# One encoder layer on one core: the Newton factor on ScalarE, and q and k scaled head by head

## The chip, the core and the metric

One core of a Trainium2 chip runs the whole layer. The core has TensorE (matrix products, PE in the profile; its weight loads are PEld), VectorE (DVE), ScalarE (ACT), GpSimd (POOL) and SyncE (SP, here only a queue of DMA issues). Each engine works through its own instructions in order and waits on semaphores for the others. The metric is the device time of one execution in microseconds (us), lower is better.

## The reference

A transformer layer on 1024 tokens of width 1024: a modulated RMS norm, one input projection, two attentions beside each other (a 2-D neighbourhood attention with 8 heads, and a dilated sliding-window attention with 12 heads in three groups), a gated merge, and a SwiGLU network. What bears on the change is the norm of q and k, over the 64 elements of a head:

```python
def rms_norm(x, g):
    x32 = x.astype(f32)
    y = x32 * lax.rsqrt(jnp.mean(x32 * x32, axis=-1, keepdims=True) + EPS)
    return (y * g.astype(f32)).astype(x.dtype)

qa = rms_norm(qa.reshape(b, s, NA_HEADS, HEAD_DIM), g_qa[l])
ka = rms_norm(ka.reshape(b, s, NA_HEADS, HEAD_DIM), g_ka[l])
...
qb = partial_rotary(rms_norm(qb.reshape(b, s, DIL_HEADS, HEAD_DIM), g_qb[l]), pos)
kb = partial_rotary(rms_norm(kb.reshape(b, s, DIL_HEADS, HEAD_DIM), g_kb[l]), pos)
```

## The kernel before

The projection to q, k and v is cut into ten units of two heads each. Units 0 to 3 are plain ("stage A" in what follows): for each of eight blocks of 128 tokens, TensorE accumulates 128 x 384 columns (q, k, v of two heads) in a bank of PSUM `pd`. Units 4 to 9 go in pairs ("stage B"): the products of two units and two token halves are formed from seven products of mixed operands instead of eight, and sums (`acc`, kept where `hT` lay) are put together by VectorE. Every float32 operand is split into a high part (`whi`, by a ScalarE copy, L129 or L1164) and a low part (`wlo`, by a subtraction, on GpSimd at L1170, on VectorE or GpSimd at L132); three matrix products replace one.

Each block of a unit ends in a post, `proj_post`, 80 in all: 32 in stage A (`acc is None`) and 48 in stage B. A post holds q and k of two heads as `qn`, 128 tokens x 4 x 64. ScalarE squares it (`sq`, L371), VectorE sums over 64 (`ss`, L375). ScalarE makes a first inverse root y as exp(-ln(ss/64 + eps)/2) (`rv`, L377 and L378), since it is not exact enough, and its square (`ry`, L379). VectorE then makes z = (ss + 64 eps) y^2 (`rz`, L380), from which one Newton step is y (1.5 - z/128). Here it is (z - 192) y (L381), times -1/128: in stage A that factor was put in when `qn` was copied out of PSUM (L373), in stage B it stands in the last product. That product (L384 or L386) takes all four heads at once, the 128x4 factor being broadcast over the 64 elements. For the dilated units GpSimd then turns 16 of the 64 elements (`ra`, `rb`, L393 to L396).

Behind the posts, TensorE transposes `qn` (L437), VectorE and ScalarE write its high and low parts (`qk`, L463 to L466), and the attention of the unit before runs between the pieces of the projection: scores (`ps_s`, L539 or L606), mask and minimum on VectorE (L553, L616, tile `st` or `sx`), exp on ScalarE (L554, L618), transposes (L565, L631), copies `PT` (L569, L638), and the product with v. VectorE also accumulates the modulation of later parts (`acc`, L337 and L339) in that time. `smix` are mixed operands fetched by DMA.

The order of TensorE's instructions is written out by hand. In this part of the program the order on VectorE, ScalarE, GpSimd and SyncE is set by a scheduler that estimates each instruction's time and follows priorities; `proj_post` has a raised one. So an edit there can move its neighbours. Behind about 600 us come the merge, the output projection and the SwiGLU network, which hold no posts.

Of the kernel before, what the change touches and what calls it, by code (L numbers as in the profile page):

```python
# [12 lines left out]
AF = mybir.ActivationFunctionType  # L13
ALU = mybir.AluOpType
# [34 lines left out]
def hybrid_layer(ctx: ExitStack, tc: tile.TileContext, x, colp, wada1, wada2, bada2, wqkv, wg, wpa, wpb,  # L49
                 wo, w1, w2, hgain, ropeg, rope, rbias, bmask, g2r, out):  # L50
    nc = tc.nc
# [47 lines left out]
    for i in (0, 2):  # L99
        nc.vector.scalar_tensor_tensor(hg[:, i:i + 1], hg[:, i:i + 1], 0.125, hg[:, i + 1:i + 2],  # L100
                                       op0=ALU.mult, op1=ALU.mult)
# [251 lines left out]
    def urgent(off):  # L353
        def deco(f):
            def g(*a):
                with tc.high_priority(off):
                    return f(*a)
            return g
        return deco

    @urgent(PP)
    def proj_post(U, t, pd=None, acc=None, here=False):
        pd = U.pd[t] if pd is None else pd
        qn = ap_.tile([128, 4, 64], F32, tag="qn", bufs=9, name="qn")
        U.qn[t] = qn
        pq = pd[:, :256].rearrange("p (h d) -> p h d", h=4)
        if acc is not None:
            nc.vector.tensor_add(qn, acc[:, :256].rearrange("p (h d) -> p h d", h=4), pq)
        v_out(U, t, pd, acc, here)
        sq = ap_.tile([128, 256], F32, tag="sq", bufs=1, name="sq")  # L370
        nc.scalar.activation(sq, pd[:, :256] if acc is None else qn.rearrange("p h d -> p (h d)"), AF.Square)  # L371
        if acc is None:
            nc.scalar.activation(qn, pq, AF.Copy, scale=-1.0 / 128)  # L373
        ss = ap_.tile([128, 4], F32, tag="ss4", bufs=2, name="ss4")
        nc.vector.tensor_reduce(ss, sq.rearrange("p (h d) -> p h d", h=4), axis=mybir.AxisListType.X, op=ALU.add)  # L375
        y, y2, z, r = (ap_.tile([128, 4], F32, tag=g, bufs=3, name=g) for g in ("rv", "ry", "rz", "rz"))
        nc.scalar.activation(y, ss, AF.Ln, scale=1.0 / 64, bias=eps)  # L377
        nc.scalar.activation(y, y, AF.Exp, scale=-0.5)  # L378
        nc.scalar.activation(y2, y, AF.Square)  # L379
        nc.vector.scalar_tensor_tensor(z, ss, 64 * EPS, y2, op0=ALU.add, op1=ALU.mult)  # L380
        nc.vector.scalar_tensor_tensor(r, z, -192.0, y, op0=ALU.add, op1=ALU.mult)  # L381
        rr = r[:, :, None].to_broadcast([128, 4, 64])
        if acc is None:
            nc.vector.tensor_tensor(qn, qn, rr, op=ALU.mult)  # L384
        else:
            nc.vector.scalar_tensor_tensor(qn, qn, -1.0 / 128, rr, op0=ALU.mult, op1=ALU.mult)  # L386
        if U.kind < 3:
            ra = ap_.tile([128, 4, 16], F32, tag="ra", bufs=2, name="ra")
            rb = ap_.tile([128, 4, 16], F32, tag="rb", bufs=2, name="rb")
            tb = U.tab[:, t]  # L390
            v4 = lambda z: z.rearrange("p (a b) c -> p a b c", a=2)
            tv = lambda f, c0, c1: tb[:, f, :, None, c0:c1].to_broadcast([128, 2, 2, c1 - c0])
            nc.gpsimd.tensor_tensor(v4(ra), v4(qn[:, :, 0:16]), tv(0, 0, 16), op=ALU.mult)  # L393
            nc.gpsimd.tensor_tensor(v4(rb[:, :, 0:8]), v4(qn[:, :, 8:16]), tv(1, 0, 8), op=ALU.mult)
            nc.gpsimd.tensor_tensor(v4(rb[:, :, 8:16]), v4(qn[:, :, 0:8]), tv(1, 8, 16), op=ALU.mult)
            nc.gpsimd.tensor_tensor(qn[:, :, 0:16], ra, rb, op=ALU.add)  # L396

    def v_out(U, t, pd, acc, here):
        if U.kind == 0:
            nc.scalar.activation(U.v[:, t, :], pd[:, 256:384], AF.Copy)  # L400
            return
        vs = acc[:, 256:384] if here else ap_.tile([128, 128], F32, tag="vs", bufs=3, name="vs")
        if acc is None:
            nc.scalar.activation(vs, pd[:, 256:384], AF.Copy)
        else:
            nc.vector.tensor_add(vs, acc[:, 256:384], pd[:, 256:384])
        vd = v_d[U.u - 2]
        if U.kind == 3:
            nc.scalar.dma_start(vd.rearrange("(c r j) d -> r j c d", c=8, r=16)[2 * t:2 * t + 2], vs)
        else:  # L410
            nc.scalar.dma_start(vd[t * 128:(t + 1) * 128, :], vs)
# [656 lines left out]
    for t in range(6):  # L1068
        proj_post(U, t)
# [13 lines left out]
    def plain_unit(u):  # L1083
        s = len(stream)
        if u > 1:
            for k in range(KT):
                def load(k=k):
                    raws[u, k] = unit_load(u, k, True)

                def split(k=k):  # L1090
                    nextw[u, k] = wsplit(raws[u, k], nc.vector if k > 1 and k % 2 else None)

                when(s - 64 + 8 * k, load)
                when(s - 36 if k < 2 else s - 8 + k, split)

        def job(t, k):
            U = unit_of(u, [nextw[u, kk] for kk in range(KT)])
            proj_chunk(U, t, k)
            if k == KT - 1:
                proj_post(U, t)  # L1100

        for t in range(8):
            for k in range(KT):
                stream.append(lambda t=t, k=k: job(t, k))
# [5 lines left out]
    def pair_evac(nm, t, pd, ua, ub):  # L1110
        if not sums:
            sums.extend(spare(q, 1536, F32) for q in range(2))
        A, B = (z[:, 384 * t:384 * t + 384] for z in sums)
        p = pd[:, :384]
        if nm == "p2":
            proj_post(unit_of(ua), t, pd, A)
        elif nm == "x4":
            proj_post(unit_of(ua), 4 + t, pd, B)
        elif nm == "w22":
            proj_post(unit_of(ub), t, pd, A, True)  # L1120
        else:
            with tc.high_priority(PP):
                if nm == "p1":
                    nc.scalar.activation(A, p, AF.Copy)
                elif nm == "x1":
                    nc.vector.tensor_add(B, A, p)
                elif nm == "x2":
                    nc.vector.tensor_add(A, A, p)
                    nc.vector.tensor_add(B, B, p)  # L1129
                else:  # L1130
                    nc.vector.tensor_add(A, A, p)
            if nm == "x3":
                proj_post(unit_of(ub), 4 + t, pd, B, True)
# [875 lines left out]
```

## Time and profile before

| | |
|---|---|
| median of 3 runs | 1483.48 us (1482.39 to 1486.61) |
| profiled execution, its own time | 1483.91 us |
| its span | 1482.1 us |
| TensorE clock granted, mean | 0.995 |
| busy: PE, DVE, ACT, POOL | 1454.2, 1112.4, 709.8, 734.3 us |
| posts | 80, from 58 to 502 us |

A row on instructions gives line, engine, operation, out<-in by the program's names, the shape, and "xN", then total busy us and the mean of one in ns, then the idle time of the engine ahead of them and what ended it; or, for one line of the code, shortest/median/longest in ns and the first and last start. A row on waits, "A <- B: us, times, longest", says that an engine stood idle ahead of A until B was done. Busy time of an instruction includes the time in which it was issued but held back by another engine.

### The profile page before, as it was taken

Reading aid. Unit: us, or ns where it says so; the run is one execution under the profiler, and the core shown is the slowest. Engines: PE = TensorE matmul, PEld = TensorE weight load, DVE = VectorE, ACT = ScalarE, POOL = GpSimd, SP = SyncE. Lnnn points to the kernel's source line nnn. Section 1 sums busy time; section 2 is a strip of 40 time slices with the busy share of each in tenths; the row PEclk is TensorE's granted clock in tenths of the full one; section 3 lists DMA queues with packets and bytes.
Section 4 is the critical chain, followed back from the end, with each engine's and each line's share of the span. In section 5 each row is a group of like instructions: output and inputs, shape, how many; then the busy total and the mean of one; then the engine's idle time right before and its main releaser. Section 6 shows DMA issues by size and latency. Waiting matters only on the chain.

```text
span 1482.1 us, 24530 instructions
## 1 busy us (share of the span) xinstructions
PE 1454.2 (98%) x8024; PEld 1238.8 (84%) x8024; DVE 1112.4 (75%) x2144; ACT 709.8 (48%) x1807; POOL 734.3 (50%) x706
## 2 busy tenths in 40 slices
PE   9999999999899999999999999999999999999998
PEld 7999998898788777888888888888888888888886
DVE  6788868878578874684877596878777777599568
ACT  5665665665678865465422353322222233354442
POOL 0353466664353544346521402677767776104464
PEclk9999999999899999999999999999999999999999
DMA  9657686775666866864374325344533334898353
GB/s 354 241 174 238 202 269 234 238 230 175 208 189 208 259 211 218 300 247 131 118 251 150 104 88 178 122 149 164 176 101 107 107 107 152 278 348 302 113 157 100
DMA packets 190416, 285.17 MB, mean 192 GB/s; under 512 B 29616, under 2 KB 91728, under 8 KB 189520
## 3 DMA queue, kind: packets, MB, share of 16 engines
q1 hardware_dynamic: 171712, 269.96, 55.0%
q10 hardware_dynamic: 18576, 13.64, 2.8%
q8 instruction: 64, 1.05, 0.3%
q14 instruction: 64, 0.52, 0.1%
HBM read 218.67 MB, written 64.86 MB: 191 GB/s over the span
## 4 chain that ended last, share of the span: by engine, by line
PE 66%; DVE 2%; issue 0%; ACT 0%; DVEq 0%
PE ps_v L1645 8%; PE ps_d L1645 8%; PE ps_s L1645 7%; PE ps_t L1645 6%; PE ps_d L840 6%; PE ps_s L1844 4%; PE ps_d L1844 4%; PE ps_t L1844 3%; PE ps_v L1844 3%; PE ps_s L1580 2%; PE ps_d L1580 2%; PE ps_v L1580 1%; PE ps_v L840 1%; PE ps_v L1431 1%; PE ps_t L1431 1%; PE ps_t L840 1%
## 5 line engine op out<-in xcount | busy, mean ns | idle before, releaser
L129 ACT ACTIVATE whi<-raw 128x512 fp32r<-128x512 f32 (+2 forms) x265 | 158.2, 608 | 178.8 <-PE ps_s L1844 37.1
L132 DVE TENSOR_TENSOR wlo<-raw,whi 128x512 fp32r<-128x512 f32 (+1 forms) x171 | 149.5, 892 | 47.5 <-ACT whi L129 44.3
L132 POOL TENSOR_TENSOR wlo<-raw,whi 128x512 fp32r<-128x512 f32 (+2 forms) x94 | 128.3, 1372 | 109.3 <-ACT whi L129 108.9
L350 PE MATMUL ps_d<-whi,hT 128*128 128x384 f32 x384 | 101.2, 338 | 0.0
L1595 POOL TENSOR_TENSOR e<-e,c 128x512 f32<-128x512 f32 x44 | 68.9, 1565 | 60.1 <-DVE c L1725 35.9
L1202 PE MATMUL ps_d<-whi,hT 128*128 128x384 f32 x328 | 94.2, 347 | 3.3 <-DVE hT L1129 2.0
L129 ACT ACTIVATE whi<-ws 128x512 fp32r<-128x512 f32 x60 | 37.7, 628 | 120.2 <-DVE ws L1662 87.1
L840 PE MATMUL ps_d<-hT,whi 128*128 128x512 f32 x256 | 81.8, 400 | 0.0
L132 POOL TENSOR_TENSOR wlo<-m,whi 128x512 fp32r<-128x512 f32 x35 | 50.7, 1455 | 52.3 <-ACT whi L129 52.3
L1202 PE MATMUL ps_d<-whi,smix 128*128 128x384 f32 x224 | 66.3, 353 | 7.8 <-DMA smix<-t_d 4.9
L1593 ACT ACTIVATE e<-e 128x512 f32<-128x512 f32 x44 | 27.4, 630 | 94.8 <-DVE e L1728 66.9
L1170 POOL TENSOR_TENSOR wlo<-raw,whi 128x384 fp32r<-128x384 f32 x48 | 51.1, 1079 | 40.0 <-ACT whi L1164 35.4
L350 PEld LDWEIGHTS ps_d<-whi,hT 128*128 128x128 f32 x384 | 69.6, 188 | 0.6 <-issue 0.6
L618 ACT ACTIVATE P<-P,st 128x256 f32<-128x256 f32 (+2 forms) x100 | 45.7, 459 | 43.2 <-DVE st L616 43.1
L1202 PEld LDWEIGHTS ps_d<-whi,hT 128*128 128x128 f32 x328 | 61.4, 192 | 4.6 <-DVE hT L1129 2.7
L350 PE MATMUL ps_d<-wlo,hT 128*128 128x384 f32 x192 | 64.2, 334 | 0.0
L1170 POOL TENSOR_TENSOR wlo<-chain,whi 128x384 fp32r<-128x384 f32 x36 | 37.5, 1055 | 49.1 <-ACT whi L1164 47.2
L1645 PE MATMUL ps_d<-h2T,whi 128*128 128x512 f32 x200 | 61.7, 389 | 0.0
L1645 PE MATMUL ps_v<-h2T,whi 128*128 128x512 f32 x192 | 59.2, 389 | 0.0
L1645 PE MATMUL ps_s<-h2T,whi 128*128 128x512 f32 x192 | 59.1, 389 | 0.0
L132 POOL TENSOR_TENSOR wlo<-gl,whi 128x512 fp32r<-128x512 f32 x30 | 40.0, 1348 | 35.1 <-ACT whi L129 35.1
L1202 PE MATMUL ps_d<-wlo,hT 128*128 128x384 f32 x164 | 55.7, 339 | 0.0
(479 smaller groups left out, 4652.9 us busy)
## 6 DMA issues: line engine op xcount, KB each, us to landing
raw<-in_w_dram SPq DMA_DIRECT2D x139, 256.0 KB, 3.5
raw<-in_wqkv_dram SPq DMA_DIRECT2D x116, 192.0 KB, 4.1
ga_d<-e SPq DMA_DIRECT2D x77, 256.0 KB, 2.5
raw<-ga_d SPq DMA_DIRECT2D x77, 256.0 KB, 3.1
smix<-t_d SPq DMA_DIRECT2D x64, 256.0 KB, 4.0
wa<-in_wada_dram SPq DMA_DIRECT2D x24, 512.0 KB, 5.1
m<-in_w_dram SPq DMA_DIRECT2D x44, 256.0 KB, 5.2
hT<-t_d SPq DMA_DIRECT2D x40, 256.0 KB, 4.8
```

The lines of the kernel that those rows point to most:

```text
L129: h = nc.scalar.activation(hi[:, :n], r, AF.Copy)
L132: (eng or nc.gpsimd).tensor_sub(lo[:, :n], r, fview(hi[:, :n]))
L350: nc.tensor.matmul(pd[:, :384], tok(a, k, t), U.w[k][b][:, :384], start=(k == 0 and i == 0), stop=(k == KT - 1 and i == 2))
L618: nc.scalar.activation(C.P[h][:nq, c], C.P[h][:nq, c], AF.Exp, scale=-1.0, bias=nm, accum_out=sm)
L840: nc.tensor.matmul(pb, w[x][:, k * 128:(k + 1) * 128], b[y][k], start=(k == 0 and q == 0), stop=(k == 3 and q == 2))
L1170: nc.gpsimd.tensor_sub(lo[:, :384], z, fview(hi[:, :384]))
L1202: nc.tensor.matmul(pd[:, :384], lhs, w[k][b][:, :384], start=(k == 0 and i == 0), stop=(k == 3 and i == 2))
L1431: nc.tensor.matmul(pb, w[a][:, j * 128:(j + 1) * 128], oT[pr][:, b, hs], start=(j == 0 and q == 0), stop=(j == len(prs) - 1 and q == 2))
L1580: nc.tensor.matmul(pbs[hf], h2T[a][:, k, t * 128:(t + 1) * 128], wow[hf, k][b], start=(n == 0 and (a, b) == PASS[0]), stop=(n == KT - 1 an ...
L1595: nc.gpsimd.tensor_mul(sg, sg, up)
L1645: nc.tensor.matmul(pb, w[p][:, k * 128:(k + 1) * 128], b[q][:, k], start=(k == 0 and i == 0), stop=(k == 3 and i == 2))
L1844: nc.tensor.matmul(pb[m], o[0][a][:, m * 128:(m + 1) * 128], o[1][b], start=(k == 0 and i == 0), stop=(k == HT - 1 and i == 2))
```

## The change

The Newton factor 1.5 - z/128 is made by a ScalarE copy with a scale and a bias (`r`, tile `rz`, L381 of the new file). `qn` is then multiplied head by head by two scalars of each partition, r and y, in one instruction for each head: four tensor_scalar of 128x64 in place of one product of 128x256 with a broadcast. The copy of `qn` out of PSUM loses its factor. The new file is three lines shorter from there on, so L1161, L1125, L1126 and L403 below are L1164, L1128, L1129 and L406 of the file before.

```diff
         if acc is None:
-            nc.scalar.activation(qn, pq, AF.Copy, scale=-1.0 / 128)
+            nc.scalar.activation(qn, pq, AF.Copy)
...
         nc.vector.scalar_tensor_tensor(z, ss, 64 * EPS, y2, op0=ALU.add, op1=ALU.mult)
-        nc.vector.scalar_tensor_tensor(r, z, -192.0, y, op0=ALU.add, op1=ALU.mult)
-        rr = r[:, :, None].to_broadcast([128, 4, 64])
-        if acc is None:
-            nc.vector.tensor_tensor(qn, qn, rr, op=ALU.mult)
-        else:
-            nc.vector.scalar_tensor_tensor(qn, qn, -1.0 / 128, rr, op0=ALU.mult, op1=ALU.mult)
+        nc.scalar.activation(r, z, AF.Copy, scale=-1.0 / 128, bias=1.5)
+        for h in range(4):
+            nc.vector.tensor_scalar(qn[:, h], qn[:, h], r[:, h:h + 1], y[:, h:h + 1], op0=ALU.mult, op1=ALU.mult)
```

TensorE's instructions stand in the same order as before. On the other engines the scheduler puts them in a new one. Three places in the first pair of units, where stage B begins; `ss_3493` of before is `ss_3589` of now, and so on through `ss_3552`/`ss_3651`, `ss_3656`/`ss_3758` and `ss_3708`/`ss_3813`: the sums of squares of four posts that follow each other.

First, VectorE at the first post of these four, before:

```order
L375 TENSOR_REDUCE ss_3493<-sq 128x4
L368 TENSOR_TENSOR qn<-hT,ps_d 128x256
L406 TENSOR_TENSOR vs<-hT,ps_d 128x128
L380 SCALAR_TENSOR_TENSOR rz<-ss_3493,ry 128x4
L381 SCALAR_TENSOR_TENSOR rz<-rz,rv 128x4
L386 SCALAR_TENSOR_TENSOR qn<-qn,rz 128x256
L375 TENSOR_REDUCE ss_3552<-sq 128x4
```

And now:

```order
L375 TENSOR_REDUCE ss_3589<-sq 128x4
L368 TENSOR_TENSOR qn<-hT,ps_d 128x256
L403 TENSOR_TENSOR vs<-hT,ps_d 128x128
L380 SCALAR_TENSOR_TENSOR rz<-ss_3589,ry 128x4
L375 TENSOR_REDUCE ss_3651<-sq 128x4
L383 TENSOR_SCALAR qn<-qn,rz,rv 128x64 x4
```

The next post's reduction has moved into the gap in which ScalarE makes the factor, and four instructions stand where one stood.

Second, VectorE at the third and fourth post, before:

```order
L380 SCALAR_TENSOR_TENSOR rz<-ss_3656,ry 128x4
L375 TENSOR_REDUCE ss_3708<-sq 128x4
L339 SCALAR_TENSOR_TENSOR acc_3692<-wa_3690,cact,acc_3692 128x512
L381 SCALAR_TENSOR_TENSOR rz<-rz,rv 128x4
L1128 TENSOR_TENSOR hT<-hT,ps_s 128x384
L1129 TENSOR_TENSOR hT<-hT,ps_s 128x384
L339 SCALAR_TENSOR_TENSOR acc_3692<-wa_3690,cact,acc_3692 128x512
L386 SCALAR_TENSOR_TENSOR qn<-qn,rz 128x256
L380 SCALAR_TENSOR_TENSOR rz<-ss_3708,ry 128x4
```

And now:

```order
L380 SCALAR_TENSOR_TENSOR rz<-ss_3758,ry 128x4
L1125 TENSOR_TENSOR hT<-hT,ps_d 128x384
L1126 TENSOR_TENSOR hT<-hT,ps_d 128x384
L339 SCALAR_TENSOR_TENSOR acc_3797<-wa_3795,cact,acc_3797 128x512
L380 SCALAR_TENSOR_TENSOR rz<-ss_3813,ry 128x4
L383 TENSOR_SCALAR qn<-qn,rz,rv 128x64 x4
```

The z of the third post is now further back, behind the evacuation that came after it, and the z of the fourth still stands behind a second evacuation and a step of `acc`.

Third, ScalarE at the same two posts, before:

```order
L377 ACTIVATE rv<-ss_3656,eps 128x4
L378 ACTIVATE rv<-rv 128x4
L379 ACTIVATE ry<-rv 128x4
L371 ACTIVATE sq<-qn 128x256
L411 DMA v_d<-vs 128x128
L377 ACTIVATE rv<-ss_3708,eps 128x4
L378 ACTIVATE rv<-rv 128x4
L379 ACTIVATE ry<-rv 128x4
L1164 ACTIVATE whi<-raw 128x384 x4
```

And now:

```order
L377 ACTIVATE rv<-ss_3813,eps 128x4
L378 ACTIVATE rv<-rv 128x4
L379 ACTIVATE ry<-rv 128x4
L381 ACTIVATE rz<-rz 128x4 x2
L1161 ACTIVATE whi<-raw 128x384 x4
```

The factors of both posts stand one after the other ahead of the four copies that make the high parts of the next weights, and the second needs the z of the fourth post.

## The prediction

> **What bounds the kernel now.** I read first the page's busy times, then the busy time of each engine in two stretches cut where the changed line runs (its 80 instances start between 61.9 and 500.0 us), then who waits for whom there.
>
> ```profile
> PE 1454.2 (98%) x8024; PEld 1238.8 (84%) x8024; DVE 1112.4 (75%) x2144; ACT 709.8 (48%) x1807; POOL 734.3 (50%) x706
> core 0: us, PE busy (x) PEld busy (x) DVE busy (x) ACT busy (x) POOL busy (x), PEclk, DMA share, GB/s
> 55.00:206.00 151.00, 151.00 (x1054) 143.99 (x1053) 118.80 (x326) 97.16 (x351) 71.91 (x146) 1.00 0.67 204
> 206.00:503.00 297.00, 277.41 (x2028) 249.04 (x2026) 233.76 (x712) 195.76 (x658) 167.20 (x207) 0.98 0.68 214
> ```
>
> TensorE bounds the whole. In stage A (55 to 206 us, 32 posts of the plain units) it never idles. In stage B (206 to 503 us, 48 posts of the paired units) it idles 19.6 of 297 us, which is most of the 28 us that it idles at all. VectorE is busy 118.8 of 151 us in A and 233.8 of 297 us in B, 79% in both: the next engine in line, executing in order. What TensorE waits for in B:
>
> ```profile
> PE ps_d L1202 <- DMA smix<-t_d: 4.9, 4, 2.9
> PE ps_d L1202 <- issue: 4.0, 2, 2.7
> PE ps_s L1202 <- DVE st L616: 3.2, 3, 1.9
> PE ps_d L1202 <- DVE hT L1129: 2.0, 2, 1.8
> PE ps_t L301 <- DVE PT L638: 1.1, 1, 1.1
> ```
>
> Columns are total us, times, longest. Three of these five name VectorE, 6.3 us: already now VectorE is at moments too late, behind its own queue. So in B VectorE time is not free. In A TensorE has no wait at all, so there VectorE time has cover. And VectorE's own idle time is in good part waiting for ScalarE (the first four rows from stage B, then two from stage A without its first 20 us):
>
> ```profile
> DVE ss L375 <- ACT sq L371: 12.9, 19, 2.8
> DVE qk L465 <- ACT qk L464: 6.5, 12, 0.9
> DVE rz L380 <- ACT ry L379: 4.5, 7, 1.2
> DVE sx L556 <- ACT P L554: 2.5, 7, 0.6
> ...
> DVE rz L380 <- ACT ry L379: 10.9, 10, 2.5
> DVE ss L375 <- ACT sq L371: 6.8, 8, 1.6
> ```
>
> **What the change removes and adds on VectorE.** Removed are one 128x4 product (L381) and one 128x256 product (L384 in A, L386 in B) for each post. First the rows of B, then those of A, then shortest, median and longest of single instructions over the whole run:
>
> ```profile
> L386 DVE SCALAR_TENSOR_TENSOR qn<-qn,rz 128x256 f32<-128x256 f32 x48 | 30.9, 644 | 0.9
> L381 DVE SCALAR_TENSOR_TENSOR rz<-rz,rv 128x4 f32<-128x4 f32 x48 | 22.0, 458 | 1.1
> L380 DVE SCALAR_TENSOR_TENSOR rz<-ss,ry 128x4 f32<-128x4 f32 x48 | 17.8, 372 | 4.5 <-ACT ry L379 4.5
> ...
> L384 DVE TENSOR_TENSOR qn<-qn,rz 128x256 f32<-128x256 f32 x32 | 15.7, 489 | 1.6
> L381 DVE SCALAR_TENSOR_TENSOR rz<-rz,rv 128x4 f32<-128x4 f32 x32 | 6.3, 196 | 0.6
> ...
> L381 DVE SCALAR_TENSOR_TENSOR rz<-rz,rv x80: 145/164/1224, 61.9 to 500.0; 128x4 f32<-128x4 f32 x80
> L380 DVE SCALAR_TENSOR_TENSOR rz<-ss,ry x80: 147/163/1065, 61.4 to 498.9; 128x4 f32<-128x4 f32 x80
> L386 DVE SCALAR_TENSOR_TENSOR qn<-qn,rz x48: 406/425/1453, 230.0 to 501.3; 128x256 f32<-128x256 f32 x48
> L384 DVE TENSOR_TENSOR qn<-qn,rz x32: 409/425/1184, 62.1 to 205.5; 128x256 f32<-128x256 f32 x32
> L375 DVE TENSOR_REDUCE ss<-sq x80: 396/416/422, 58.7 to 496.6; 128x4 f32<-128x256 f32 x80
> ```
>
> The means are far above the shortest, while the reduction L375 never is. One place shows why, VectorE's three rows first, then GpSimd's:
>
> ```profile
> 228.15 0.88 DVE L380 SCALAR_TENSOR_TENSOR rz<-ss,ry 128x4 f32<-128x4 f32 x1
> 229.07 0.93 DVE L381 SCALAR_TENSOR_TENSOR rz<-rz,rv 128x4 f32<-128x4 f32 x1
> 230.04 1.18 DVE L386 SCALAR_TENSOR_TENSOR qn<-qn,rz 128x256 f32<-128x256 f32 x1
> ...
> 228.00 2.94 POOL L1170 TENSOR_TENSOR wlo<-chain,whi 128x384 fp32r<-128x384 f32 x3
> ```
>
> Three GpSimd instructions of 0.98 us run one after the other, and each of the three VectorE instructions ends just after one of them: the two engines take turns, instruction by instruction. So what counts is also how many such instructions VectorE issues.
>
> Added are four tensor_scalar of 128x64 with two scalars per partition. No such shape is in the trace. The nearest rows, and two of the last of them back to back:
>
> ```profile
> L251 DVE TENSOR_SCALAR xd<-ident,xs x4: 281/284/288, 9.3 to 13.5; 128x128 f32<-128x128 f32 x4
> L337 DVE TENSOR_SCALAR acc<-wa,cact x6: 477/478/586, 77.2 to 308.5; 128x512 f32<-128x512 f32 x6
> L969 DVE TENSOR_SCALAR yT<-yT,sc x16: 535/546/1106, 22.5 to 54.1; 128x512 f32<-128x512 f32 x16
> ...
> 27.85 1.00 DVE L969 TENSOR_SCALAR yT<-yT,sc 128x512 f32<-128x512 f32 x2
> ```
>
> L251 and L337 have one scalar operand: (477 - 281)/384 = 0.51 ns an element. L969 has two: 535 - 477 = 58 ns more. So 128x64 with two is 281 - 64 x 0.51 + 58 = 306 ns. Two L969 end after 1.00 us, not 1.09, so the next starts 0.09 us before the end of one. Four occupy 4 x (0.306 - 0.09) = 0.86 us of VectorE, undisturbed. L969 also reaches 1106 ns, so tensor_scalar takes turns with GpSimd too.
>
> With the turns, stage B: the old pair costs 0.458 + 0.644 - 0.08 (overlap) = 1.02 us. The turn costs 0.31 us at L381 (458 - 145), 0.24 at L386 (644 - 406), 0.22 at L380 (372 - 147). I take 0.24 for each of the four, L386 being the instruction that they replace: 0.86 + 4 x 0.24 = 1.82 us, +0.80 a post, 48 x 0.80 = +38 us. Ends: no turns at all gives 0.86 - 1.02 = -0.16, or -8 us; 0.31 for each gives +1.08, or +52 us. Stage A: old 0.196 + 0.489 - 0.08 = 0.60; turns cost 0.05 (L381) to 0.08 (L384), so new 0.86 + 4 x 0.06 = 1.10, +0.50 a post, +16 us over 32 posts (ends +8 and +19).
>
> [...]
>
> **What it adds as waits.** The factor goes to ScalarE: 80 more ACTIVATE of 128x4, like L379:
>
> ```profile
> L379 ACT ACTIVATE ry<-rv x80: 188/206/238, 61.1 to 498.4; 128x4 f32<-128x4 f32 x80
> ```
>
> 80 x 0.206 = 16.5 us on an engine that is busy 293 of 448 us in A and B together: the duration itself is covered by its idle time. But the path is now VectorE, ScalarE, VectorE where it was VectorE alone. In 25 of the 80 posts the order puts the tensor_scalar right behind the z instruction, so VectorE stands for the whole trip; elsewhere a reduction or other work lies between. The new wait is unknown: its nearest rows are those of 4.5 us (L380) and 12.9 us (L375) in B; I take 9 in B, and 6 in A by the number of posts. Ends 0 and 13 each. On ScalarE the new instruction stands in front of others: in 23 posts it is directly ahead of the copies L1164 that make the weights' high parts, on which GpSimd (L1170) and then TensorE wait. At the third place of the order shown above two of them now precede four such copies:
>
> ```profile
> 240.17 1.75 ACT L1164 ACTIVATE whi<-raw 128x384 fp32r<-128x384 f32 x4
> 240.75 4.54 POOL L1170 TENSOR_TENSOR wlo<-raw,whi 128x384 fp32r<-128x384 f32 x4 [1.65 <-ACT whi L1164]
> 243.39 0.96 DVE L380 SCALAR_TENSOR_TENSOR rz<-ss,ry 128x4 f32<-128x4 f32 x1
> 249.08 0.33 PE L1202 MATMUL ps_d<-whi,hT 128*128 128x384 f32 x1
> ```
>
> The copies started at 240.17 and TensorE used the result from 249.08; GpSimd was done at 245.3, so 3.8 us of room. The second z ran at 243.39 to 244.35; behind it the copies start 4.2 us later, and the room is gone by 0.4 us. I put +4 us for such places in B, with 0 and +20 as ends (20 is 21 product starts at about 1 us each).
>
> The dropped scale of the copy L373 and the merged branches change no instruction's size: nothing. TensorE's order is unchanged; SyncE's differs by a few neighbours that swap places, priced at nothing since the landings they carry are needed many us later; if that cover fails it shows as more of the 4.9 us wait for smix.
>
> **The sum.** Stage B: VectorE 233.8 + 38 = 272 us of work, plus its waits for ScalarE 12.9 + 6.5 + 4.5 + 2.5 = 26 us, plus the new 9: 307 us in a stretch of 297, so +10. (Its waits for TensorE I let go: they vanish when VectorE is late.) Stage A by the same sum: 118.8 + 16 + 17.7 + 6 = 158.5 of 151, +7.5; but TensorE never waits there, and such waits shrink when VectorE falls behind, so I take +4. ScalarE's queue +4. Together +18 us on the profiled execution's 1483.9 us (its span is 1482.1; the median of the runs is 1483.48): **1502 us**. What is late next, after VectorE, are the weights' low parts on GpSimd.
>
> **Rivals.** (1) VectorE and the chain both overflow: 0.31 us a turn (+52), waits 13 in B gives 234 + 52 + 26 + 13 = 325, +28; A its full +7.5; ScalarE's queue +10: 1529 us. For it: turns cluster, as at 228 us; against it: GpSimd is busy only 56% of B. (2) It stays hidden: ScalarE's waits on the VectorE side melt by 26 us as VectorE falls behind, and 272 fits in 297: 1484 to 1488 us. The same time comes out if the four cost what the pair costs, 0.255 us each in B. For it: TensorE has 100% in A; against it: 6.3 us of waits for VectorE already now, and the prices above. [...] (3) Faster: the tensor_scalar are short enough to slip between GpSimd's instructions. Then VectorE gains 8 us in B and up to the 6.3 us of TensorE's waits for it go: about 1478 us. It decides where four of them occupy less than the 1.02 us of the old pair, under 0.255 us each; undisturbed they take 0.215, so this needs a turn cost under 0.04 us, where the rows show 0.22 to 0.31.
>
> **Chances.** My case (1490 to 1515 us) 0.52, rival 1 0.18, rival 2 0.18, rival 3 0.12. The likeliest gives 1502. About 0.3%, 4.5 us, is what a measurement of this kernel can tell from no change. Slower: 0.52 + 0.18 + a small part of rival 2 = 0.73; same 0.15; faster 0.12. The range from 1480 to 1530 leaves out most of rival 3 and the part of rival 1 beyond 1529, near 0.18.
>
> **What would show it.** In the profile after: 320 tensor_scalar with a shortest near 0.30 us and a mean in B near 0.5; VectorE busy near 272 us in what was stage B; a new row of VectorE waiting for ScalarE's rz; more TensorE idle, named st, hT, PT or whi, before 520 us; from then on the same lengths as now. I am wrong if the tensor_scalar take under 0.25 us, if TensorE's idle time in B stays near 20 us with VectorE above 90%, or if the change in time comes from behind 503 us.

## The result, and the profile after

The changed kernel takes 1520.32 us (median, 1513.53 to 1525.81) where the kernel before took 1483.11 us on the same chip: a ratio of 1.0249, 95% interval 1.0219 to 1.0279. It is slower, by 37 us. The profiled execution took 1521.67 us, its span is 1519.9 us. Its first line on the page, and the busy time of the engines in four stretches, first of the changed kernel, then of the kernel before (columns as in the first fence of the prediction). The cuts are the first plain projection, the first and the last matmul of the paired projections, and the first matmul of the merge:

```profile
PE 1468.8 (97%) x8024; PEld 1246.0 (82%) x8024; DVE 1158.5 (76%) x2304; ACT 720.6 (47%) x1887; POOL 734.8 (48%) x706
61.50:202.20 140.70, 139.52 (x987) 132.28 (x986) 123.40 (x366) 92.72 (x350) 71.01 (x140) 1.00 0.65 198
202.20:528.00 325.80, 287.69 (x2002) 256.01 (x2001) 261.06 (x790) 197.94 (x695) 158.85 (x206) 0.95 0.62 197
528.00:725.60 197.60, 194.94 (x1078) 155.38 (x1077) 131.19 (x264) 116.17 (x261) 107.98 (x81) 1.00 0.67 230
725.60:1519.90 794.30, 789.61 (x3525) 652.95 (x3523) 602.77 (x781) 281.07 (x508) 392.14 (x269) 1.00 0.48 160
```

```profile
60.50:199.70 139.20, 139.20 (x986) 132.19 (x985) 113.12 (x313) 89.79 (x325) 69.19 (x142) 1.00 0.66 201
199.70:494.00 294.30, 274.92 (x2001) 248.80 (x2000) 228.78 (x699) 192.87 (x652) 161.96 (x205) 0.98 0.69 218
494.00:688.00 194.00, 193.79 (x1079) 155.30 (x1078) 127.74 (x249) 115.05 (x254) 107.11 (x81) 1.00 0.67 233
688.00:1482.10 794.10, 789.46 (x3524) 652.58 (x3523) 602.64 (x781) 279.34 (x506) 391.45 (x268) 1.00 0.48 160
```

The second column is the length. The start is 1.0 us later, the plain stretch 1.5 longer, the paired stretch 31.5, the next one 3.6, the rest 0.2: together 37.8 us, the difference of the spans. So five sixths of the loss are in the paired stretch. There TensorE idles 38.1 us where it idled 19.4, and the same 2000 matmuls or so keep it busy 12.8 us longer. The mean granted clock, third from the end, is 0.95 there, against 0.98.

The added instructions: the groups of the paired stretch and of the plain one, then all instances of each with shortest, median and longest:

```profile
L383 DVE TENSOR_SCALAR qn<-qn,rz,rv 128x64 f32<-128x64 f32 x185 | 87.6, 535 | 5.8 <-ACT rz L381 5.7
...
L383 DVE TENSOR_SCALAR qn<-qn,rz,rv 128x64 f32<-128x64 f32 x124 | 36.5, 355 | 3.6 <-ACT rz L381 3.5
...
L383 DVE TENSOR_SCALAR qn<-qn,rz,rv x320: 285/308/1396, 63.0 to 542.4; 128x64 f32<-128x64 f32 x160
L381 ACT ACTIVATE rz<-rz x80: 188/205/231, 62.7 to 539.7; 128x4 f32<-128x4 f32 x80
```

What TensorE waits for in the paired stretch (total, times, longest):

```profile
PE ps_s L1199 <- DVE st L613: 7.2, 2, 5.8
PE ps_d L1199 <- ACT whi L1161: 5.6, 4, 2.2
PE ps_d L1199 <- issue: 3.7, 2, 2.6
PE ps_s L603 <- DVE hT L403: 3.5, 1, 3.5
PE ps_t L562 <- ACT P L554: 2.8, 4, 1.0
```

VectorE leads the list. The longest of these waits, 5.8 us, in the timeline (start, length, engine, line, count), VectorE's row first, then GpSimd's, then TensorE's:

```profile
349.95 7.49 DVE L383 TENSOR_SCALAR qn<-qn,rz,rv 128x64 f32<-128x64 f32 x8 [0.20 <-ACT rz L381]
...
349.62 1.01 POOL L1156 TENSOR_TENSOR chain<-raw,chain 128x384 f32<-128x384 f32 x1
350.65 2.93 POOL L1167 TENSOR_TENSOR wlo<-raw,whi 128x384 fp32r<-128x384 f32 x3
353.54 1.01 POOL L1156 TENSOR_TENSOR chain<-raw,chain 128x384 f32<-128x384 f32 x1
354.50 0.99 POOL L1167 TENSOR_TENSOR wlo<-raw,whi 128x384 fp32r<-128x384 f32 x1
355.45 1.94 POOL L1156 TENSOR_TENSOR chain<-raw,chain 128x384 f32<-128x384 f32 x2
...
353.77 0.34 PE L1199 MATMUL ps_d<-whi,smix 128*128 128x384 f32 x1
359.90 0.69 PE L1199 MATMUL ps_s<-whi,hT 128*128 128x384 f32 x1 [5.79 <-DVE st L613]
360.38 0.52 PE L1199 MATMUL ps_s<-wlo,hT 128*128 128x384 f32 x1
```

The eight tensor_scalar of two posts stand together. GpSimd has eight instructions in a row, about 0.96 us apart, and each tensor_scalar lets one of them go first: 7.49 us for work that would take 8 x 0.22 = 1.8 us undisturbed, by my estimate from two at 63.00 us, where GpSimd is idle: 0.53 us together, 0.308 for one. VectorE's reads of PSUM (L1125, L1126) and the masks (L613) stand behind the block, so TensorE has nothing until 359.90. A 128x384 product then takes 0.52 or 0.69 us in place of 0.34, since the clock has dropped. Two stretches at the stop, TensorE's busy time behind the length, the granted clock third from the end:

```profile
349.90:357.90 8.00, 4.21 (x45) 3.65 (x45) 7.95 (x10) 1.88 (x6) 7.48 (x8) 1.00 0.79 184
357.90:364.70 6.80, 4.80 (x15) 4.80 (x16) 4.82 (x24) 4.79 (x20) 1.00 (x1) 0.50 0.27 83
```

The clock is half for 6.8 us after the stop. In the records of the clock, the paired stretch has 34.1 us at half rate, where the kernel before had 13.7. TensorE was busy in 30.9 of these us, before in 12.8. Work of 18.1 us at half rate would take half of that at full rate, so by my estimate about 9 us were lost: most of the 12.8 us that TensorE is busy longer. No matmul runs in the 3.4 us before 357.9, and the stretches at 0.50 are 3.4 or 6.8 us long. But the stop was not as long in the other places. Ahead of the other seven half-rate stretches of the pairs, TensorE was busy for 0.8 to 1.8 of the 3.4 us before, as in this window, behind which the clock is half for 3.4 us:

```profile
456.88:460.29 3.41, 1.71 (x12) 1.41 (x12) 3.38 (x13) 0.91 (x2) 1.35 (x2) 1.00 0.70 235
```

So the clock also fell behind stops that left only part of such a stretch idle. It did not behind each: in the kernel before, TensorE was busy for 1.61 us from 481.20 to 484.61, and the clock stayed at 1.00.

### The profile page after: what moved, and what is told of

It is laid out like the page before. It is cut to its first block, busy times and chain, and to the rows that moved or that the text cites. A ratio compares the mean times of both kernels' runs of the same rounds, so it can differ in the third digit from the quotient of the medians.

```text
span 1519.9 us, 24821 instructions
## 1 busy us (share of the span) xinstructions
PE 1468.8 (97%) x8024; PEld 1246.0 (82%) x8024; DVE 1158.5 (76%) x2304; ACT 720.6 (47%) x1887; POOL 734.8 (48%) x706
## 4 chain that ended last, share of the span: by engine, by line
PE 73%; DVE 10%; DMA 5%; issue 2%; ACT 2%; POOL 1%; SPq 0%; ACTq 0%; POOLq 0%; DVEq 0%
PE ps_v L1642 7%; PE ps_d L1642 7%; PE ps_s L1642 7%; PE ps_t L1642 6%; PE ps_d L837 5%; PE ps_d L1199 3%; DVE qn L383 3%; PE ps_s L1841 3%; PE ps_d L1841 3%; PE ps_d L350 3%; PE ps_t L1841 3%; PE ps_v L1841 3%; PE ps_d L1577 2%; PE ps_s L1577 2%; DMA raw<-in_wqkv_dram 2%
## 5 line engine op out<-in xcount | busy, mean ns | idle before, releaser
L383 DVE TENSOR_SCALAR qn<-qn,rz,rv 128x64 f32<-128x64 f32 x320 | 129.0, 464 | 11.0 <-ACT rz L381 10.9
L129 ACT ACTIVATE whi<-ws 128x512 fp32r<-128x512 f32 x60 | 37.7, 628 | 118.0 <-DVE ws L1659 75.4
```

Source lines behind the costliest of these rows:

```text
L129: h = nc.scalar.activation(hi[:, :n], r, AF.Copy)
L383: nc.vector.tensor_scalar(qn[:, h], qn[:, h], r[:, h:h + 1], y[:, h:h + 1], op0=ALU.mult, op1=ALU.mult)
```

## The experiments

"Factor on ScalarE" is called the trip below. In each short diff the minus lines are those of the kernel the experiment starts from, and n is the executions behind the median. One table first, of the paired stretch in one profiled execution each, from its first to its last matmul. The last column is the sum of VectorE's waits for ScalarE and for TensorE there, over the rows of the view of waits.

| kernel | length | TensorE idle | at half clock | VectorE busy | waits of VectorE: ScalarE + TensorE |
|---|---|---|---|---|---|
| before | 294.2 | 19.4 | 13.7 | 228.7 | 29.7 + 30.6 |
| changed | 325.6 | 38.1 | 34.1 | 261.1 | 30.0 + 30.7 |
| trip alone | 297.5 | 19.7 | 17.1 | 224.2 | |
| heads alone | 317.5 | 33.1 | 30.7 | 265.0 | 22.9 + 24.8 |
| changed, without turns | 293.0 | 14.6 | 16.2 | 230.9 | 26.6 + 31.4 |
| heads without turns, no trip, old factor | 292.1 | 19.2 | 3.4 | 245.0 | 18.8 + 24.3 |
| the change in the paired units alone | 323.8 | 37.7 | 30.7 | 255.7 | 30.1 + 32.8 |
| last version | 285.6 | 15.2 | 3.4 | 233.8 | 19.5 + 27.8 |

**The trip alone.** ScalarE makes z - 192, VectorE multiplies by y, and the broadcast product stays.

```
-        nc.vector.scalar_tensor_tensor(r, z, -192.0, y, op0=ALU.add, op1=ALU.mult)
+        nc.scalar.activation(r, z, AF.Copy, bias=-192.0)
+        nc.vector.tensor_tensor(r, r, y, op=ALU.mult)
```

> The trip alone: ScalarE makes z - 192 (one more 128x4 ACTIVATE for each post), VectorE multiplies it by y (128x4) and scales q and k with one broadcast product as before. VectorE's instructions are as many and as large as before. Theory 1 (the time goes into VectorE's work: four instructions that each take turns with GpSimd): little is lost, 1482 to 1490 us, TensorE idle in the paired units near 20 us. Theory 2 (the trip VectorE-ScalarE-VectorE and the copies queued behind it on ScalarE): most of the 37 us, 1505 to 1520 us. Theory 3 (any new order that the scheduler makes costs): no relation to what is added, a time anywhere between 1475 and 1515 us.

1491.3 us (n 5), ratio 1.0047 (1.003 to 1.0064), +7.4 us. In the paired stretch:

```profile
201.60:499.20 297.60, 277.87 (x2002) 249.84 (x2001) 224.25 (x691) 195.99 (x689) 161.14 (x204) 0.97 0.68 217
L382 DVE TENSOR_TENSOR rz<-rz,rv 128x4 f32<-128x4 f32 x47 | 18.2, 387 | 5.2 <-ACT rz L381 4.9
```

The new wait is there, 4.9 us, nearly as long as in the changed kernel (5.7), and the stretch grows by 3.3 us. The trip alone gives a fifth of the loss, a little more than theory 1 allowed and far less than theory 2 asked for.

**The four tensor_scalar alone.** VectorE keeps the factor, as a tensor_scalar of 128x4, and L373 has no scale, as in the changed kernel.

```
-        nc.vector.scalar_tensor_tensor(r, z, -192.0, y, op0=ALU.add, op1=ALU.mult)
...
-            nc.vector.scalar_tensor_tensor(qn, qn, -1.0 / 128, rr, op0=ALU.mult, op1=ALU.mult)
+        nc.vector.tensor_scalar(r, z, -1.0 / 128, 1.5, op0=ALU.mult, op1=ALU.add)
+        for h in range(4):
+            nc.vector.tensor_scalar(qn[:, h], qn[:, h], r[:, h:h + 1], y[:, h:h + 1], op0=ALU.mult, op1=ALU.mult)
```

> Head by head without the trip: VectorE itself makes 1.5 - z/128 (a 128x4 tensor_scalar with two constants), then the four 128x64 tensor_scalar. Theory 1: VectorE has all the work of the changed kernel and the factor on top (48 x about 0.35 us in the paired units), so it is as slow as the changed kernel or slower, 1510 to 1535 us. Theory 2: the trip is gone and with it most of the loss, 1484 to 1497 us.

1515.4 us (n 4), ratio 1.022 (1.0187 to 1.0254), +31.5 us: without the trip, five sixths of the loss.

```profile
202.40:520.00 317.60, 284.49 (x2001) 254.45 (x2000) 265.10 (x842) 192.59 (x650) 159.36 (x207) 0.95 0.64 204
L383 DVE TENSOR_SCALAR qn<-qn,rz,rv 128x64 f32<-128x64 f32 x189 | 76.9, 468 | 1.0
```

**The number of instructions.** The kernel before, its broadcast product cut into two of two heads each.

```
-        rr = r[:, :, None].to_broadcast([128, 4, 64])
+        for h in (0, 2):
+            rr, qh = r[:, h:h + 2, None].to_broadcast([128, 2, 64]), qn[:, h:h + 2]
```

> The kernel before with its one broadcast product cut into two of 128x2x64, no trip, no tensor_scalar. Theory 1: one more VectorE instruction for each post, about 0.08 us of fixed time after overlap and 0.24 us of turn with GpSimd, 48 x 0.3 = 15 us of VectorE in the paired units; if VectorE's work goes into the time one for one, as between the two kernels (32 us of work, 31 us of stage), 1493 to 1501 us. Theory 2: nothing is added to the path through ScalarE, 1481 to 1487 us.

1494.81 us (n 4), ratio 1.0071 (1.0051 to 1.0091), +10.9 us. In the paired stretch:

```profile
200.50:504.00 303.50, 278.17 (x2002) 249.97 (x2001) 242.56 (x742) 193.28 (x652) 163.38 (x207) 0.97 0.67 215
L387 DVE SCALAR_TENSOR_TENSOR qn<-qn,rz 128x128 f32<-128x128 f32 x92 | 46.4, 544 | 0.9
```

The same elements through twice the instructions: each half takes 544 ns on average against 634 for the whole in the same stretch, and the stretch is 9 us longer. Splitting costs time with the old instruction too.

**The turns taken away.** A tensor_scalar that also writes an accumulated sum stands in the trace as another instruction, TENSOR_SCALAR_CACHE_REDUCE. With two scalars it leaves q and k scaled differently from the reference: the layer's output was off by a relative 0.87 in three of the four kernels with it and by 0.18 in the fourth, so of them only the time is read. First with the changed kernel and the sums in the tile kind of ss:

```
+        ja = ap_.tile([128, 4], F32, tag="ss4", bufs=2, name="ja")
-            nc.vector.tensor_scalar(qn[:, h], qn[:, h], r[:, h:h + 1], y[:, h:h + 1], op0=ALU.mult, op1=ALU.mult)
+            nc.vector.tensor_scalar(qn[:, h], qn[:, h], r[:, h:h + 1], y[:, h:h + 1], op0=ALU.mult, op1=ALU.mult, accum_out=ja[:, h:h + 1])
```

> The changed kernel with an accumulated sum written out of each of the four tensor_scalar (the sums are not used; the scaling itself may come out differently, so only the time is read). [...] If the turns are what makes the four dear, the mean of one in the paired units falls from 0.535 to about 0.36 us and VectorE's work there by 48 x 4 x 0.18 = 34 us: 1485 to 1500 us. If the number of instructions with their fixed time, or the trip, is the cause, 1512 to 1530 us. If the form takes turns like the other, the mean stays near 0.5 us and the time near 1520 us.

1510.09 us (n 4), ratio 1.0166 (1.0134 to 1.0197): 26 us slower than before, so taken alone it would clear the turns of most of the loss. But the trace has a stop that no other kernel has, one wait of TensorE in the plain stretch:

```profile
L384 DVE TENSOR_SCALAR_CACHE_REDUCE qn<-qn,rz,rv x320: 321/335/342, 62.7 to 530.7; 128x64 f32<-128x64 f32 x160
...
PE ps_d L350 <- ACT qn L373: 9.0, 1, 9.0
```

None of the 320 takes longer than 342 ns, so the turns are gone. The stop of 9.0 us is new: the sums take one of the two buffers of ss, and the next post's reduction must wait for a post's last tensor_scalar. The run mixes two things and settles nothing alone.

So again with a tile of its own for the sums, three buffers:

```
-        ja = ap_.tile([128, 4], F32, tag="ss4", bufs=2, name="ja")
+        ja = ap_.tile([128, 2], F32, tag="sc", bufs=3, name="ja")
```

> As the kernel with the accumulated sums, but the sums lie in a tile of their own, not among the two buffers of ss, so that posts do not wait for each other through it (the scaling itself is still not the reference's, only the time is read). Turns as the cause: the single stop of 9 us in the plain units goes, VectorE's work in the paired units stays near 226 us, and the paired units take 295 to 302 us: 1488 to 1500 us. If the trip or the fixed time of four instructions were what costs, the paired units would stay above 310 us and the time above 1508 us.

1485.35 us (n 10), ratio 1.0019 (1.0004 to 1.0034): +1.5 us. The same trip, the same four instructions a post on the same operands, and nearly the whole loss is gone. In the paired stretch, and the group there:

```profile
201.20:494.30 293.10, 278.54 (x2002) 250.00 (x2001) 230.99 (x977) 197.54 (x696) 160.06 (x208) 0.97 0.69 221
L384 DVE TENSOR_SCALAR_CACHE_REDUCE qn<-qn,rz,rv 128x64 f32<-128x64 f32 x188 | 54.9, 333 | 6.0 <-ACT rz L381 6.0
L384 DVE DVE_READ_ACCUMULATOR qn<-qn,rz,rv 128x1 f32 x188 | 15.2, 81 | 0.0
```

333 ns on average where the changed kernel has 535, although the form is 25 ns dearer than the median of the other (308) and reads an accumulator besides; and the wait for the trip is still there, 6.0 us. The loss is therefore the turns with GpSimd, which also are VectorE's longer busy time, 261 us against 231. Shortest, median and longest of the 320 are 285/308/1396 ns in the changed kernel, 321/335/342 in the first run with the sums and 315/333/373 in this one, where GpSimd is busy for 160 of the 293 us. Why one form takes turns and the other does not, no run shows.

**Is it VectorE's total time?** Two kernels add VectorE work and no turns: the form without turns and no trip, once with the factor by tensor_scalar,

```
-        nc.scalar.activation(r, z, AF.Copy, scale=-1.0 / 128, bias=1.5)
+        nc.vector.tensor_scalar(r, z, -1.0 / 128, 1.5, op0=ALU.mult, op1=ALU.add)
```

> Neither trip nor turns: the four tensor_scalar with accumulated sums (the scaling is not the reference's, only the time is read), and the factor made by VectorE. Turns as the cause, the trip a small part: 3 to 8 us below the same kernel with the trip, 1482 to 1495 us. If the trip mattered only together with the turns: the same as with the trip within 3 us. If the count of instructions matters: above 1500 us.

and once with the 128x4 product of the kernel before:

```
-        rr = r[:, :, None].to_broadcast([128, 4, 64])
...
-            nc.vector.scalar_tensor_tensor(qn, qn, -1.0 / 128, rr, op0=ALU.mult, op1=ALU.mult)
+        for h in range(4):
+            nc.vector.tensor_scalar(qn[:, h], qn[:, h], r[:, h:h + 1], y[:, h:h + 1], op0=ALU.mult, op1=ALU.mult, accum_out=ja[:, h % 2:h % 2 + 1])
```

> The kernel before (its L381 on VectorE, no trip), with the last product as four tensor_scalar with accumulated sums, which take no turns (the scaling is not the reference's, only the time is read). VectorE has fewer turns than before but more work: the four occupy about 1.2 us where the product occupied 0.56, so 48 x 0.64 = 30 us more in the paired units, 259 in all. If it is VectorE's time as such that the stage follows, whatever it is made of: 20 to 30 us over before, 1503 to 1514 us. If the turns do the harm by holding up GpSimd and the weights' low parts: near before, 1482 to 1492 us.

1494.37 us (n 4), ratio 1.0075 (1.005 to 1.01), and 1492.56 us (n 5), ratio 1.0063 (1.004 to 1.0085). Their paired stretches:

```profile
201.00:502.00 301.00, 279.63 (x2008) 251.37 (x2006) 246.96 (x1028) 192.64 (x649) 159.15 (x207) 0.97 0.67 214
...
203.10:495.30 292.20, 273.01 (x2001) 245.01 (x2001) 245.05 (x1020) 190.10 (x640) 157.22 (x205) 0.99 0.68 218
```

VectorE is busy 18 and 16 us longer than before, with nearly the same work; one stretch is 7 us longer and the other 2 us shorter. In the second, VectorE's waits fell by 17 us (table): the added work went into them. But that execution, 1487.7 us, is the fastest of its five, at a granted clock of 0.999; the other four had 0.993 to 0.995 and took 2 to 7 us longer. By their medians the two kernels are 10.5 and 9.4 us slower than before, and 2 to 3 us of that lie in the plain stretch (141.4 and 141.9 us in the profiles against 139.2). The second is just above the range expected of the turns and well below that of VectorE's total time. The first is 9 us slower than the same kernel with the trip, where I expected it to be 3 to 8 us faster; why stays open. So VectorE's added time costs something without turns too, about 10 us here, with whatever a new order does in it (below). The changed kernel adds twice as much, 32 us, and loses 37; no kernel here adds as much without turns.

**Where it is lost.** The change in the plain units alone (first lines), and in the paired units alone (second); the other units keep the lines of the kernel before:

```
         if acc is None:
-            nc.vector.tensor_tensor(qn, qn, rr, op=ALU.mult)
+            nc.scalar.activation(r, z, AF.Copy, scale=-1.0 / 128, bias=1.5)
+            for h in range(4):
+                nc.vector.tensor_scalar(qn[:, h], qn[:, h], r[:, h:h + 1], y[:, h:h + 1], op0=ALU.mult, op1=ALU.mult)
...
+        if acc is not None:
+            nc.scalar.activation(r, z, AF.Copy, scale=-1.0 / 128, bias=1.5)
+            for h in range(4):
+                nc.vector.tensor_scalar(qn[:, h], qn[:, h], r[:, h:h + 1], y[:, h:h + 1], op0=ALU.mult, op1=ALU.mult)
```

> The change in the plain units alone (32 posts), the paired units as before. VectorE has about 10 us more work there of 140 us and TensorE never waits there: 1484 to 1488 us, against 1502 if half of the loss came from these units.

> The change in the paired units alone (48 posts); the plain units keep the kernel before. Theory of turns in streaks (the four tensor_scalar meet rows of GpSimd instructions where the paired units mix weights): all of the loss is here, since the change in the plain units alone gave 1487.8: 1512 to 1522 us, tensor_scalar mean near 0.53 us there, half rate of TensorE 25 to 35 us in that stage. Rival, an adding up of both stages (VectorE falls behind in the plain units already and carries the lateness over): 1500 to 1508, clearly under the full change.

Plain units alone: 1487.8 us (n 10), ratio 1.0029 (1.0015 to 1.0044), +3.9 us. Paired units alone: 1519.06 us (n 4), ratio 1.0221 (1.0205 to 1.0238), +33.2 us. They add up to 37, the change's whole loss. Of the second:

```profile
60.70:199.90 139.20, 139.20 (x986) 132.19 (x985) 113.37 (x314) 90.49 (x327) 69.68 (x143) 1.00 0.66 201
199.90:523.80 323.90, 286.16 (x2002) 255.09 (x2001) 255.72 (x778) 195.88 (x687) 157.36 (x203) 0.95 0.62 197
L384 DVE TENSOR_SCALAR qn<-qn,rz,rv 128x64 f32<-128x64 f32 x180 | 83.6, 526 | 6.2 <-ACT rz L382 6.1
```

The plain stretch is that of the kernel before, the paired one that of the changed kernel. The adding up of lateness from one stretch to the next is refuted.

**The order by itself.** The kernel before with the posts' priority in the scheduler at 0: the same instructions in another order.

```
-PP, QT, AQ, AT, AV = 100, 0, 0, 0, 0
+PP, QT, AQ, AT, AV = 0, 0, 0, 0, 0
```

> The kernel before with the posts' priority set to 0, so that the scheduler puts the same instructions in another order. Theory 3, a new order costs by itself: more than 5 us away from 1483, in either direction. Theory 1: the same work on VectorE and so within 5 us of it.

1488.8 us (n 10), ratio 1.0026 (1.0013 to 1.0039). An order that nothing else forces moves the time by 5 us. Differences of this size between the kernels here may be the order's alone, the +1.5, +3.9 and +7.4 among them. The order differs between the kernels of the other experiments too, so it was not held fixed in them. But the instruction sorts them: the three with the plain tensor_scalar in the pairs are 31 to 37 us slower than before, and the four with the other form and no stop of 9 us (the last is below) lie between 7 us faster and 10.5 us slower.

**Less VectorE work.** ScalarE makes the whole factor, (z - 192)y, one head at a time; VectorE keeps one product.

```
-        nc.vector.scalar_tensor_tensor(r, z, -192.0, y, op0=ALU.add, op1=ALU.mult)
+        nc.scalar.activation(m, y, AF.Copy, scale=-192.0)
+        for h in range(4):
+            nc.scalar.activation(r[:, h:h + 1], z[:, h:h + 1], AF.Identity, scale=y[:, h:h + 1], bias=m[:, h:h + 1])
```

> A version that takes a turn away from the kernel before: ScalarE makes (z - 192) y head by head (four 128x1 ACTIVATE with scale and bias per partition, and one for -192 y), VectorE keeps only z and the one broadcast product. VectorE loses 0.46 us a post, 22 us in the paired units; ScalarE gains five instructions of about 0.2 us, 48 us there, of 100 idle. If less work on VectorE goes into the time as more work did: 1465 to 1478 us. If VectorE at 229 of 294 us is no longer what the stage follows, and the trip costs as in the trip alone: 1484 to 1495 us.

1510.84 us (n 5), ratio 1.0189 (1.0166 to 1.0212). VectorE does 22 us less in the paired stretch and the kernel is 28 us slower, beyond both ranges that I gave:

```profile
205.40:515.40 310.00, 283.27 (x2002) 253.23 (x2001) 206.67 (x645) 241.84 (x866) 161.57 (x207) 0.96 0.65 207
...
PE ps_d L1205 <- ACT whi L1167: 10.5, 4, 3.3
```

ScalarE, 49 us busier, now delays the copies that the weights need. It has less to give than its 66% share suggests.

**A version from this.** Without trip and turns, in the paired units alone: the factor takes in the scales of the kernel before, so that one scalar a head is enough. With one scalar q and k are scaled as in the reference.

```
-        nc.scalar.activation(y2, y, AF.Square)
+        nc.scalar.activation(y2, y, AF.Square, scale=1.0 if acc is None else 128 ** -0.5)
-        nc.vector.scalar_tensor_tensor(r, z, -192.0, y, op0=ALU.add, op1=ALU.mult)
+        nc.vector.scalar_tensor_tensor(r, z, -192.0 if acc is None else -1.5, y, op0=ALU.add, op1=ALU.mult)
-            nc.vector.scalar_tensor_tensor(qn, qn, -1.0 / 128, rr, op0=ALU.mult, op1=ALU.mult)
+            for h in range(4):
+                nc.vector.tensor_scalar(qn[:, h], qn[:, h], r[:, h:h + 1], None, op0=ALU.mult, op1=ALU.add,
+                                        accum_out=ja[:, h % 2:h % 2 + 1])
```

> The kernel before, with the broadcast product of the paired units replaced by four tensor_scalar of 128x64 with one scalar that also write an accumulated sum, the form that took 333 us x 10^-3 each and never longer beside GpSimd; no trip to ScalarE, the two small factors stay on VectorE. Theory of turns: VectorE's work rises by 48 x (4 x 0.36 - 0.64) = 38 us at most in the paired units, but no turns are added, so 1480 to 1490. Theory of total VectorE time (272 us of work in 297, as much as in the changed kernel): 1495 to 1505.

1478.67 us (n 5) beside 1485.85, ratio 0.9955 (0.9942 to 0.9968): 7 us faster than the kernel before, a little under the range that I gave. That is little more than an order alone moved (5 us), so it is not shown that the missing turns gain it. Its five executions were granted 0.997 to 1.000 of the clock, the kernel before beside them 0.992 to 0.995. The paired stretch, its group, and one post in the timeline:

```profile
200.40:486.00 285.60, 270.43 (x2001) 244.46 (x2000) 233.84 (x1002) 190.29 (x643) 158.00 (x204) 0.99 0.70 224
L388 DVE TENSOR_SCALAR_CACHE_REDUCE qn<-qn,rz 128x64 f32<-128x64 f32 x180 | 42.4, 273 | 0.8
...
229.13 0.94 DVE L381 SCALAR_TENSOR_TENSOR rz<-rz,rv 128x4 f32<-128x4 f32 x1
230.10 0.28 DVE L388 TENSOR_SCALAR_CACHE_REDUCE qn<-qn,rz 128x64 f32<-128x64 f32 x1
230.31 0.09 DVE L388 DVE_READ_ACCUMULATOR qn<-qn,rz 128x1 f32 x1
230.31 0.28 DVE L388 TENSOR_SCALAR_CACHE_REDUCE qn<-qn,rz 128x64 f32<-128x64 f32 x1
```

L381 still takes its turn (0.94 us), the four behind it do not, and one starts every 0.20 us. VectorE is busy 5 us longer than before and the stretch is 8.6 us shorter. My price of 0.36 us for each step was too high by 0.16; with it VectorE would have reached 272 us, so this run does not test the rival of the total time. The two above test it with half the amount.

## Why the prediction was right, and where it was wrong

Slower was right, and the time lies in the range, 18 us above the number given. It is outside my own case (1490 to 1515) and nearer to rival 1, so the range held because rival 1 was in it. The step that failed is in the sum of stage B.

- **Price and turns: held.** Shortest 285 and median 308 ns stood against 306; mean 535 in the paired stretch against 0.5 us, 355 in the plain one. VectorE is busy 261 us there, 272 foretold. From start to start two of them are 0.22 us apart (0.53 us for the two at 63.00 us, less 0.308), where 0.306 - 0.09 was foretold.
- **"Its waits for TensorE I let go: they vanish when VectorE is late": failed.** VectorE waits 30.7 us for TensorE in the changed kernel, 30.6 before. Its waits for ScalarE, 30.0 with the new one in them, did not grow in sum. Work and waits together make up the stretch, 261 + 61 = 322 of 325.6 us. The prediction's own numbers with that term kept, 272 + 26 + 9 + 31 = 338, overshoot by 12, since work, ScalarE's waits and the new wait came smaller. Stage B was therefore +31.5 and not +10. Part of why they stayed the trace shows: the longest of them lies where TensorE is not late but busy. It is 6.0 us long and ends at 319.6; the kernel before has it too, 4.6 us, to 303.5. In both, TensorE works without a gap at full clock, on products that stand ahead of VectorE's next scores in its written order, and VectorE has nothing (columns as before, the changed kernel first):

```profile
313.60:319.59 5.99, 5.99 (x52) 5.67 (x52) 0.00 (x0) 2.01 (x5) 4.45 (x7) 1.00 0.51 178
298.85:303.46 4.61, 4.61 (x44) 4.29 (x44) 0.00 (x0) 2.81 (x8) 4.11 (x5) 1.00 0.93 286
```

  As I read it, the lateness comes in blocks: a block of VectorE's stops TensorE, both are late by it, and the wait behind it is as long as ever. Two stretches of the changed kernel in which, by the chain that ended last, the tensor_scalar alone set the end:

```profile
351.64 5.80 DVE qn L383 x6
508.14 4.46 DVE qn L383 x4
```

  Work that was added without turns went into the waits in one execution (table, sixth row), but by the medians not all of it. That 16 us cost 10 and 32 us cost 37 could also be a bound on the amount; no run separates that from the blocks, so the blocks are a reading of single places, while it is shown that the turns cause the loss.
- **TensorE's clock: not in the sum.** 20.4 us more at half rate, by the estimate above about 9 of the 31.5 us.
- **Stage A +4: near.** The plain stretch grew by 1.5 us and began 1.0 later; alone the change there cost 3.9. TensorE's cover held, as argued.
- **ScalarE's queue +4: right in size.** TensorE's waits for whi came to 5.6 us. The new wait of VectorE was 5.7 us in the paired stretch, 9 foretold.
- **"From then on the same lengths as now": nearly.** The stretch behind the pairs grew by 3.6 us. It also did so in the last version, where the pairs were shorter (197.5 us against 194.0, from the same marks), so its cause is not the lateness of the pairs. It stays open.
- **Rivals.** Rival 1 (1529) had the size more nearly right, through "turns cluster", but with 0.31 us for a turn where the mean over the median is 535 - 308 = 0.23. Rival 2's waits hardly melted: those for ScalarE fell from 29.7 to 24.3 us, and the new one of 5.7 took their place; without turns and trip they fell to 18.8. Rival 3 needed tensor_scalar that slip between GpSimd's; in the other form they took no turns (longest 291 ns in the last version), and the last version was 7 us faster.

## What to carry to other kernels

Count the instructions that take turns with GpSimd, not their elements: beside a row of GpSimd instructions about 0.96 us apart each cost up to one of those here (eight took 7.49 us), and several in a row held up everything queued behind them (TensorE for 5.8 us). Do not let an engine's waits pay for its added work without asking where they lie: some are there because the other engine is busy (6.0 us here). Look for the longest block, for what stands behind it, and for a drop of TensorE's clock after it (0.50 for 6.8 us here). Where scaling per head is wanted, the form of tensor_scalar that writes a sum, in a buffer of its own, took no turns here (longest 291 ns with one scalar, against 1396 in the changed kernel); use it with one scalar, since with two the scaling came out differently.

## What was not expected of the hardware

A second scalar per partition cost about 60 ns also in the form with the sum (median 335 ns in the first run with it, 274 in the last version). The reading of the accumulator, 82 ns in the last version, lies inside the overlap of neighbours: with one scalar, tensor_scalar of 128x64 start 0.20 us apart although each is recorded with 0.28 + 0.09 us. And the changed kernel's clock went to half behind stretches of 3.41 us in which TensorE had been busy for up to 1.81 us.
